# The output layer of an encoder block as seven half-size products, with sums of its weights made in DRAM

## The chip, the cores and the metric

The kernel runs on one core of a Trainium2 chip. The metric is the device time of one execution in microseconds (us). Three runs of the kernel before took 958.44 to 965.11 us, median 962.56 us. The engines are named as in the profile: PE (TensorE) multiplies matrices into PSUM, DVE (VectorE) and ACT (ScalarE) work element by element, POOL (GpSimd) does small things and issues some DMAs, SP (SyncE) issues most DMAs.

## The reference

One layer of an encoder: a token mixer, then a SwiGLU feed-forward layer, each between norms, with a residual sum. The change concerns the feed-forward layer, above all its last product:

```python
def swiglu(h, w_gate, w_up, w_down):
    return (jax.nn.silu(h @ w_gate) * (h @ w_up)) @ w_down
...
    h = rmsnorm(x, pre_ffn_gain[l])
    f = swiglu(h, w_gate[l], w_up[l], w_down[l])
    x = x + rmsnorm(f, post_ffn_gain[l])
```

Everything is float32. `h` is 1024 x 1024 (rows x features), `w_gate` and `w_up` 1024 x 2816, `w_down` 2816 x 1024.

## The kernel before

All matrices are split into a high and a low part (`split`, line 105: a cast on ACT, line 107, and a subtraction on DVE, line 110). `mm3` (line 133) multiplies in three matmuls: high x high (L135), high x low (L137), low x high (L139).

**Hidden layer (about 345 to 715 us).** There are 22 iterations `n`, alternately a block of `w_gate` (n even) and of `w_up` (n odd), for the 11 pairs of 128-wide chunks `p_` and `p_ + 11` of the 2816 features. Each iteration is already computed as seven products of half size over sums of its operands. `begin(n)` makes products 1 and 2, `rest(n)` the products 5, 6, 3, 7 and 4; each has 12 matmuls, an iteration 84. Sums of products are accumulated in one PSUM bank, and ACT copies intermediate values out (`copied`, L971) before the next product is added on top. DVE adds two of them (`plus`, L988). For even n the four results (1,1), (1,2), (2,2), (2,1) are gates (L980, L981). For odd n they are multiplied with the gates (L984), giving the activations, and POOL's DMA queue writes them ("spills") to `act_d` in DRAM (L985), 256 KB each. All these values live in `pt` tiles, 12 buffers.

The weights of iteration n come in two tiles `raw` of 512 KB (`wload`, L779 and L780 on SP's queue; three buffers). A tile is loaded when its buffer is free, which is when DVE has split or added its old contents, so DVE's order decides when a load starts. `unit1` splits the first tile (ACT's cast of `wh`), `unit2` and `unit3` form sums (L929, L733), `unit4` splits a quarter (`sh<-raw`). ACT runs its instructions in order: a cast that waits for a load holds up the copies behind it.

**Output layer (about 715 to 951 us).** For each half `dh` of the 1024 output columns, 8 PSUM banks hold the 8 row tiles `t`. For each of the 22 chunks, `operands` loads the chunk of `w_down` (`dr`, 256 KB, L1079) and of `act_d` (`ar`, 512 KB, L1081) and splits both; 8 x 3 matmuls follow. The last four chunks are taken row tile by row tile, so that a tile ends every 12 matmuls and `first_half` or `second_half` (norm, gain, residual, output DMA; L1105 to L1113) runs beside the next one. 22 x 8 x 2 x 3 = 1056 matmuls.

The code is written in program order; a scheduler orders the instructions on each engine's queue, and within a queue they run in that order.

## Time and profile before

| what | value |
|---|---|
| median of three runs | 962.56 us (958.44 to 965.11) |
| profiled execution, its own time | 964.13 us |
| span of the profiled execution | 962.3 us |
| PE busy | 945.6 us, 98% of the span |
| DVE, ACT, POOL busy | 559.6, 396.5, 87.8 us |
| DMA | 117.04 MB, mean 122 GB/s |

The profile is of one execution. Busy time is the time in which an engine had an instruction running; matmuls overlap, so 98% of busy PE means that it was never left waiting, not that it ran at its peak. A row of the timeline gives the start in us, the duration in us, the engine, the line, the operation, output<-inputs with shapes, and in square brackets the idle time just before it and what ended that.

### The profile page before, as it was taken

What the parts mean: (1) busy time and instruction counts of PE and PEld (TensorE: products, weight loads), DVE (VectorE), ACT (ScalarE), POOL (GpSimd) and SP (SyncE); (2) the same over time, 40 slices, a digit from 0 to 9 for tenths busy, and PEclk for the clock granted to TensorE, in tenths of its full rate; (3) what the DMA queues carried; (4) which work ended last, traced back from release to release, by engine and by line L of the source; (5) the groups of instructions that cost most, each with busy time, mean ns of one, the idle gap of its engine ahead of it and who ended that gap; (6) DMA issues with size and microseconds to landing.
All of it is one profiled execution on the core that took longest, in us unless ns stands there. A gap on an engine that the chain in (4) does not pass through costs nothing.

```text
span 962.3 us, 11186 instructions
## 1 busy us (share of the span) xinstructions
PE 945.6 (98%) x4240; PEld 780.7 (81%) x4240; DVE 559.6 (58%) x824; ACT 396.5 (41%) x677; POOL 87.8 (9%) x115
## 2 busy tenths in 40 slices
PE   9999999989998999999999999999999999999996
PEld 7888888878886888888888888888888888888885
DVE  4367694636588867666567656656556333533306
ACT  6433523527776534333333433333345223633201
POOL 0020113202132000000000000000000000000001
PEclk9999999989999999999999999999999999999999
DMA  8522031514246133223122221231069634254107
GB/s 331 205 67 66 6 110 45 197 66 131 88 143 223 73 121 112 75 69 129 55 77 92 95 77 66 88 110 55 33 236 328 255 132 160 79 187 165 56 1 262
DMA packets 37733, 117.04 MB, mean 122 GB/s; under 512 B 4752, under 2 KB 5424, under 8 KB 37680
## 3 DMA queue, kind: packets, MB, share of 16 engines
q1 hardware_dynamic: 31248, 95.32, 29.1%
q0 software_dynamic: 6288, 20.99, 5.6%
q8 instruction: 33, 0.54, 0.2%
q14 instruction: 20, 0.16, 0.0%
q10 hardware_dynamic: 144, 0.02, 0.0%
HBM read 94.80 MB, written 21.51 MB: 121 GB/s over the span
## 4 chain that ended last, share of the span: by engine, by line
PE 89%; DVE 4%; DMA 2%; POOL 1%; ACT 1%; issue 1%; DVEq 0%; POOLq 0%; ACTq 0%
PE ps L139 28%; PE ps L135 28%; PE ps L137 28%; PE ps L249 5%; DVE wl L110 1%; DMA t<-rg_d 1%; POOL lrs L158 1%; PE ps L189 1%; PE ps L740 1%; DMA raw<-in_x 0%; DMA raw<-in_tables 0%; DMA rg_d<-t 0%; DVE L L110 0%; ACT y L447 0%; POOL mst L851 0%
## 5 line engine op out<-in xcount | busy, mean ns | idle before, releaser
L137 PE MATMUL ps<-hl_t,sh 128*128 128x512 f32 x352 | 137.1, 389 | 0.0
L137 PE MATMUL ps<-dl,ah 128*128 128x512 f32 x352 | 137.1, 389 | 0.0
L139 PE MATMUL ps<-dh,al 128*128 128x512 f32 x352 | 137.1, 389 | 0.0
L135 PE MATMUL ps<-hh_t,sh 128*128 128x512 f32 x352 | 137.1, 389 | 0.0
L135 PE MATMUL ps<-dh,ah 128*128 128x512 f32 x352 | 137.1, 389 | 0.0
L110 DVE TENSOR_TENSOR al<-ar,ah 128x1024 fp32r<-128x1024 f32 x44 | 53.8, 1224 | 103.2 <-ACT ah L107 103.0
L110 DVE TENSOR_TENSOR t<-t,sh 128x1024 fp32r<-128x1024 f32 x42 | 51.5, 1225 | 92.5 <-ACT sh L107 92.5
L139 PE MATMUL ps<-hh_t,t 128*128 128x512 f32 x252 | 98.1, 389 | 0.0
L107 ACT CAST ah<-ar 128x1024 fp32r<-128x1024 f32 x44 | 46.0, 1051 | 111.1 <-PE ps L137 101.1
L107 ACT CAST sh<-t 128x1024 fp32r<-128x1024 f32 x42 | 44.2, 1052 | 90.0 <-PE ps L137 51.5
L988 DVE TENSOR_TENSOR pt<-ps,pt 128x512 f32<-128x512 f32 x88 | 60.4, 687 | 33.2 <-PE ps L139 32.6
L137 PEld LDWEIGHTS ps<-hl_t,sh 128*128 128x128 f32 x352 | 66.1, 188 | 13.8
L135 PEld LDWEIGHTS ps<-dh,ah 128*128 128x128 f32 x352 | 66.1, 188 | 13.8
L139 PEld LDWEIGHTS ps<-dh,al 128*128 128x128 f32 x352 | 66.1, 188 | 13.8
L135 PEld LDWEIGHTS ps<-hh_t,sh 128*128 128x128 f32 x352 | 66.1, 188 | 13.6
L137 PEld LDWEIGHTS ps<-dl,ah 128*128 128x128 f32 x352 | 66.1, 188 | 13.5
L107 ACT CAST wh<-raw 128x1024 fp32r<-128x1024 f32 x40 | 41.9, 1051 | 82.5 <-PE ps L137 21.3
L971 ACT COPY pt<-ps 128x512 f32<-128x512 f32 x88 | 51.2, 582 | 58.8 <-PE ps L139 58.8
L135 PE MATMUL ps<-hh_b,wh 128*128 128x512 f32 x176 | 69.6, 395 | 1.8 <-ACT wh L107 1.5
L139 PE MATMUL ps<-hh_b,wl 128*128 128x512 f32 x176 | 68.8, 393 | 1.0 <-DVE wl L110 1.0
L137 PE MATMUL ps<-hl_b,wh 128*128 128x512 f32 x176 | 69.3, 394 | 0.0
L135 PE MATMUL ps<-xh,wh 128*128 128x512 f32 x160 | 64.1, 401 | 0.0
(248 smaller groups left out, 1771.6 us busy)
## 6 DMA issues: line engine op xcount, KB each, us to landing
ar<-act_d SPq DMA_DIRECT2D x44, 512.0 KB, 3.7
raw<-in_w_gate SPq DMA_DIRECT2D x24, 512.0 KB, 4.0
raw<-in_w_up SPq DMA_DIRECT2D x24, 512.0 KB, 3.2
act_d<-pt POOLq DMA_DIRECT2D x44, 256.0 KB, 2.3
dr<-in_w_down SPq DMA_DIRECT2D x44, 256.0 KB, 3.7
raw<-in_w_feat SPq DMA_DIRECT2D x10, 512.0 KB, 3.7
t<-in_x SPq DMA_DIRECT2D x8, 512.0 KB, 8.6
raw<-in_w_out SPq DMA_DIRECT2D x8, 512.0 KB, 3.8
```

Of the source, the lines that this page charges most:

```text
L107: nc.scalar.copy(h, src)
L110: nc.vector.tensor_tensor(l, src, f(h), op=ALU.subtract)
L135: nc.tensor.matmul(ps, ah, bh, start=first, stop=False, skip_group_check=resumed)
L137: nc.tensor.matmul(ps, ah, bl, start=False, stop=False, skip_group_check=resumed)
L139: nc.tensor.matmul(ps, al, bh, start=False, stop=last, skip_group_check=resumed)
L158: nc.gpsimd.tensor_tensor(dst, t, mhalf[:, 0:1].broadcast_to([P, w]), op=ALU.pow)
L189: nc.tensor.matmul(warm, ones[:, 0:P], ones, start=True, stop=True)
L249: nc.tensor.matmul(uvps[t], (lk if p_ == 2 else hk)[:, ts_], (wl if p_ == 1 else wh)[:, c], start=k == 0 and p_ == 0, stop=k == NK - 1 and ...
L740: nc.tensor.transpose(tps[k // 4][:, (k % 4) * P : (k % 4 + 1) * P], hv[:, k, :], ident)
L971: copies.append(nc.scalar.copy(v, ps).ins)
L988: nc.vector.tensor_tensor(v, ps, v, op=ALU.add)
```

## The change

The output layer is computed like the hidden layer: seven products of half size instead of eight. With the activations and `w_down` cut into quarters, the left operands are `a11`, `a12`, `a22` and the sums `s3 = a11 - a21`, `s1 = a21 - a22`, `s2 = s1 - a11`, `s4 = s2 + a12`; the right operands are the quarters B11, B21, B22 and the sums `u1`, `u2`, `u3`, `u4`. Four things change:

1. In `done`, odd iterations form the four left sums on DVE (44 instructions of 128 x 512) and spill seven values per pair instead of four.
2. The right sums are made in DRAM, for six groups of two chunks (the last has one): SP copies four quarters of `w_down` into `u1`..`u4` (`copy_sums`), and POOL issues adding DMAs, two from `w_down` and two from one sum into another (`add_sums`).
3. The output layer runs seven products (`product_out`), each with 11 chunks x 4 row tiles x 3 matmuls, 924 in all. It loads 512 KB of left and 512 KB of right operand for each group of two chunks. The last two groups of a product are taken row tile by row tile.
4. The first group's operands are loaded and split during the last hidden-layer iteration (`head`). The order of two operand tiles in `hh` and `hl` is swapped, and the pools of the output layer are laid out anew.

```diff
-    act_d = drp.tile([NF, P, S], F32, name="act_d")
+    GR = [(p_, min(p_ + 2, NP)) for p_ in range(0, NP, 2)]
+    a_d = {q: grouped(q) for q in ("a11", "a12", "a22", "s1", "s2", "s3", "s4")}
+    b_d = {q: grouped(q) for q in ("u1", "u2", "u3", "u4")}
...
+    def spill(q, p_, v):
+        nc.gpsimd.dma_start(a_d[q][p_ // 2][:, (p_ % 2) * HALF : (p_ % 2 + 1) * HALF], v)
...
+        nc.vector.tensor_tensor(c, c, gates.pop((i, j)), op=ALU.mult)
+        if (i, j) == (1, 1):
+            acts["a11", p_] = c
+            spill("a11", p_, c)
+        elif (i, j) == (1, 2):
+            acts["a21"] = c
+            s3 = pt()
+            sub(s3, acts["a11", p_], c)
+            spill("s3", p_, s3)
+        elif (i, j) == (2, 2):
+            spill("a22", p_, c)
+            s1 = acts.pop("a21")
+            sub(s1, s1, c)
+            spill("s1", p_, s1)
+            s2 = acts["s2"] = pt()
+            sub(s2, s1, acts.pop(("a11", p_)))
+            spill("s2", p_, s2)
         else:
-            nc.vector.tensor_tensor(c, c, gates.pop((i, j)), op=ALU.mult)
-            nc.gpsimd.dma_start(act_d[p_ + (i - 1) * NP, :, (j - 1) * HALF : j * HALF], c)
+            spill("a12", p_, c)
+            s4 = pt()
+            nc.vector.tensor_tensor(s4, acts.pop("s2"), c, op=ALU.add)
+            spill("s4", p_, s4)
...
+    def copy_sums(g):
+        for q, w in (("u1", B11), ("u3", B12), ("u2", B22), ("u4", B21)):
+            nc.sync.dma_start(chunks(b_d[q][g]), halves_of(w, g))
+
+    def add_sums(g, q):
+        if q in ("u1", "u3"):
+            v = halves_of(B12 if q == "u1" else B22, g)
+            nc.gpsimd.dma_start(chunks(b_d[q][g]), v, accum_op=ALU.add)
+        else:
+            nc.gpsimd.dma_start(b_d[q][g], b_d["u1" if q == "u2" else "u2"][g], accum_op=ALU.add, max_dma_last_dim=1024)
...
+        if n == len(kinds) - 1:
+            head("a11", B11)
         rest(n)
+        g, j = divmod(n - 4, 3)
+        if 0 <= g < len(GR):
+            if j == 0:
+                with tc.issue_after(loads[n + 2]):
+                    copy_sums(g)
+            for q in (("u1",), ("u3", "u2"), ("u4",))[j]:
+                add_sums(g, q)
...
+        product_out("a11", B11, Xb, True, keep("v1", Xb))
+        product_out("a12", B21, Yb, True, c11)
+        product_out("s2", "u2", Xb, False, keep("u2", Xb))
+        product_out("s1", "u1", Zb, True, keep("v5", Zb))
+        product_out("s3", "u3", Xb, False, c22)
+        product_out("s4", B22, Zb, False, c12)
+        product_out("a22", "u4", Xb, False, c21)
```

How the instructions move is shown at three places. The first is DVE's queue at the end of an odd iteration, before. L988 adds products, L984 multiplies with a gate, L110 with `sh` and `raw` is the split of `unit4` that frees a `raw` buffer:

```order
L929 TENSOR_TENSOR t_696_4584<-raw_4516 128x512
L984 TENSOR_TENSOR pt_4434<-pt_4434,pt_4298 128x512
L988 TENSOR_TENSOR pt_4486<-ps_4496,pt_4486 128x512
L110 TENSOR_TENSOR sh_4512<-raw_4383,sh_4512 128x512
L984 TENSOR_TENSOR pt_4486<-pt_4486,pt_4351 128x512
L733 TENSOR_TENSOR t_696_4584<-t_696_4584,raw_4515 128x512
```

The same place now (the lines have moved: L936 was L929, L1002 was L984, L1071 was L988, L740 is a subtraction, here of `s1` and `s2`, L1022 is `s4`):

```order
L936 TENSOR_TENSOR t_717_4748<-raw_4675 128x512
L1002 TENSOR_TENSOR pt_4583<-pt_4583,pt_4446 128x512
L1071 TENSOR_TENSOR pt_4637<-ps_4652,pt_4637 128x512
L740 TENSOR_TENSOR pt_4597<-pt_4597,pt_4583 128x512
L1002 TENSOR_TENSOR pt_4637<-pt_4637,pt_4499 128x512
L740 TENSOR_TENSOR pt_4644<-pt_4597,pt_4548 128x512
L110 TENSOR_TENSOR sh_4671<-raw_4531,sh_4671 128x512
L1022 TENSOR_TENSOR pt_4668<-pt_4644,pt_4637 128x512
L740 TENSOR_TENSOR t_717_4748<-t_717_4748,raw_4674 128x512
```

Between the last sum of products and the split of `raw` stand three instructions where none stood.

The second place is POOL's queue in the iteration n = 7 and the one after it (odd, the first chunk pair of whose group is 2; in `a112_d` the tensor is `a11`, the group starts at chunk 2). L992 is a spill, L1066 an add from `w_down`, L1068 an add from one sum to another:

```order
L992 DMA a112_d_109<-pt_552_3692 128x512
L1066 DMA u12_d_151<-in_w_down 256x1x512
L1066 DMA u32_d_163<-in_w_down 256x1x512
L1068 DMA u22_d_157<-u12_d_151 512x256
L992 DMA s32_d_139<-pt_563_3766 128x512
L1068 DMA u42_d_169<-u22_d_157 512x256
L992 DMA a222_d_121<-pt_557_3727 128x512
L992 DMA s12_d_127<-pt_558_3741 128x512
L992 DMA a122_d_115<-pt_564_3781 128x512
L992 DMA s22_d_133<-pt_565_3788 128x512
L992 DMA s42_d_145<-pt_569_3812 128x512
```

Where four spills followed each other, spills now stand behind adds, and each of the last two adds reads what the add before it wrote. Groups 1, 3 and 5 are placed like this, in odd iterations; groups 0, 2 and 4 have their four adds in a row in an even iteration.

The third place is SP's queue at the copies of that group, behind the weight loads of iteration 9:

```order
L786 DMA raw_571_3818<-in_w_up 128x1024
L787 DMA raw_572_3819<-in_w_up 128x1024
L1061 DMA u12_d_151<-in_w_down 256x1x512
L1061 DMA u32_d_163<-in_w_down 256x1x512
L1061 DMA u22_d_157<-in_w_down 256x1x512
L1061 DMA u42_d_169<-in_w_down 256x1x512
L786 DMA raw_594_3960<-in_w_gate 128x1024
```

Four copies of 512 KB now stand between two weight loads, once in three iterations.

## Rows read from the trace of the kernel before

**Rows 1.** Page, parts 1 and 2: busy us, and the granted clock by slice.

```profile
PE 945.6 (98%) x4240; PEld 780.7 (81%) x4240; DVE 559.6 (58%) x824; ACT 396.5 (41%) x677; POOL 87.8 (9%) x115
...
PEclk9999999989999999999999999999999999999999
```

**Rows 2.** Page, part 4: the chain that ended last, shares by engine, by line.

```profile
PE 89%; DVE 4%; DMA 2%; POOL 1%; ACT 1%; issue 1%; DVEq 0%; POOLq 0%; ACTq 0%
PE ps L139 28%; PE ps L135 28%; PE ps L137 28%; PE ps L249 5%; DVE wl L110 1%; DMA t<-rg_d 1%; POOL lrs L158 1%; PE ps L189 1%; PE ps L740 1%; DMA raw<-in_x 0%; DMA raw<-in_tables 0%; DMA rg_d<-t 0%; DVE L L110 0%; ACT y L447 0%; POOL mst L851 0%
```

**Rows 3.** Windows: the hidden layer, the output layer, the tail, three stretches inside.

```profile
core 0: us, PE busy (x) PEld busy (x) DVE busy (x) ACT busy (x) POOL busy (x), PEclk, DMA share, GB/s
345.00:715.10 370.10, 370.10 (x1635) 306.65 (x1634) 231.27 (x314) 139.83 (x199) 21.60 (x40) 1.00 0.26 89
715.10:951.50 236.40, 236.40 (x1045) 195.87 (x1044) 96.74 (x127) 77.75 (x118) 4.35 (x8) 1.00 0.47 164
951.50:962.30 10.80, 2.61 (x12) 1.83 (x10) 4.73 (x9) 1.36 (x4) 1.08 (x2) 0.85 0.52 196
...
720.00:730.00 10.00, 10.00 (x45) 8.27 (x44) 6.17 (x8) 4.85 (x7) 0.00 (x0) 1.00 1.00 353
...
740.00:750.00 10.00, 10.00 (x46) 8.29 (x45) 4.41 (x5) 3.14 (x4) 0.00 (x0) 1.00 0.92 335
...
770.00:790.00 20.00, 20.00 (x90) 16.58 (x89) 7.30 (x8) 5.23 (x8) 0.00 (x0) 1.00 0.40 139
```

**Rows 4.** Page, part 5: the output layer's matmuls (count, busy us, mean ns).

```profile
L137 PE MATMUL ps<-dl,ah 128*128 128x512 f32 x352 | 137.1, 389 | 0.0
L139 PE MATMUL ps<-dh,al 128*128 128x512 f32 x352 | 137.1, 389 | 0.0
...
L135 PE MATMUL ps<-dh,ah 128*128 128x512 f32 x352 | 137.1, 389 | 0.0
```

**Rows 5.** Timeline, PE: product 3 of an even iteration; first and last output-layer matmul.

```profile
535.07 0.39 PE L135 MATMUL ps<-hh_b,sh 128*128 128x512 f32 x1
...
714.59 0.39 PE L135 MATMUL ps<-dh,ah 128*128 128x512 f32 x1
...
953.72 0.39 PE L139 MATMUL ps<-dh,al 128*128 128x512 f32 x1
```

**Rows 6.** Timeline, DVE: first and last of four instructions for one row tile's end.

```profile
949.49 0.22 DVE L1106 TENSOR_SCALAR fst<-fst 128x1 f32<-128x1 f32 x1 [0.44 <-ACT junk L1105]
...
951.03 0.75 DVE L1110 SCALAR_TENSOR_TENSOR fy<-fy,fst,xr 128x512 f32<-128x512 f32 x1
```

**Rows 7.** Timeline, DVE, SP and ACT: from an odd hidden-layer iteration to an even one.

```profile
525.51 0.68 DVE L988 TENSOR_TENSOR pt<-ps,pt 128x512 f32<-128x512 f32 x1
526.11 0.68 DVE L110 TENSOR_TENSOR sh<-raw,sh 128x512 fp32r<-128x512 f32 x1
...
526.82 0.33 SPq L779 DMA_DIRECT2D raw<-in_w_gate  x1
529.23 0.33 SPq L780 DMA_DIRECT2D raw<-in_w_gate  x1
546.02 0.33 SPq L779 DMA_DIRECT2D raw<-in_w_up  x1
...
530.37 1.05 ACT L107 CAST wh<-raw 128x1024 fp32r<-128x1024 f32 x1 [2.68 <-DMA raw<-in_w_gate]
...
532.55 0.59 ACT L971 COPY pt<-ps 128x512 f32<-128x512 f32 x1 [0.59 <-PE ps L139]
```

**Rows 8.** Page, part 3: SP's queue and POOL's queue (packets, MB, share of 16 engines' span).

```profile
q1 hardware_dynamic: 31248, 95.32, 29.1%
q0 software_dynamic: 6288, 20.99, 5.6%
```

**Rows 9.** Page, part 6: fastest and slowest 512 KB loads (count, size, us to landing).

```profile
raw<-in_w_up SPq DMA_DIRECT2D x24, 512.0 KB, 3.2
...
t<-in_x SPq DMA_DIRECT2D x8, 512.0 KB, 8.6
```

More of the change, by code (lines that the diff above doesn't have):

```diff
@@ new lines, in tile_encoder_layer, with head @@
+    heads = {}
+    def head(a, b):
+        rb, ra = raw(), raw()
+        get(a, b, 0, ra, rb)
+        o = []
+        for r in (rb, ra):
+            h, l = t4r(), t4r()
+            split(h, l, r)
+            o += [h, l]
+        heads[a, 0] = o
+    def copy_sums(g):
[5 more added lines that the diff above has]
+            nc.gpsimd.dma_start(chunks(b_d[q][g]), v, accum_op=ALU.add)
+        else:
+            nc.gpsimd.dma_start(b_d[q][g], b_d["u1" if q == "u2" else "u2"][g], accum_op=ALU.add, max_dma_last_dim=1024)
@@ new lines, in mm, with product_out @@
+        def mm(ps, t, o, j, first, last, resumed):
+            bh_, bl_, ah_, al_ = o
+            ts_ = slice(j * HALF + t * P, j * HALF + (t + 1) * P)
+            js = slice(j * HALF, (j + 1) * HALF)
+            mm3(ps, ah_[:, ts_], al_[:, ts_], bh_[:, js], bl_[:, js], first, last, resumed=resumed)
+        def product_out(a, b, banks, fresh, then):
+            n = len(GR)
+            for g in range(n - 2):
+                o = operands(a, b, g)
+                for j in range(2):
+                    for t in TT:
+                        mm(banks[t], t, o, j, fresh and g == 0 and j == 0, False, not fresh)
+            os = [operands(a, b, g) for g in (n - 2, n - 1)]
+            for t in TT:
+                for o, w in zip(os, (2, 1)):
+                    for j in range(w):
+                        mm(banks[t], t, o, j, False, w == 1, not fresh)
+                then(t)
```

140 lines of the change are left out of this document (83 added, 57 removed).

## The prediction

> **What bounds the kernel now.** I read the page's busy times, then the chain that ended last, then the windows, then single rows of the timeline. TensorE is busy 98% of the span at a granted clock of 9 tenths or more in every slice [rows 1]. The chain is TensorE for 89%; the three lines of `mm3` alone hold 84% [rows 2]. The windows divide this: from 345 us to 715.1 us (hidden layer) and from 715.1 us to 951.5 us (output layer) TensorE never idles, at clock 1.00; only the tail, 951.5 to 962.3 us, is something else [rows 3]. VectorE is busy 63% of the hidden layer and 41% of the output layer, ScalarE 38% and 33%, the DMA engines 26% and 47%. So a matmul taken out saves its full pitch, unless what is added makes TensorE wait where it now never does. The second question decides this case, since all the added work lies in windows where something must stay hidden.
>
> **What is removed.** The output layer has 1056 matmuls (8 row tiles, 2 halves, 22 chunks, 3 terms), three groups of 352 [rows 4]. The busy time of one, 389 ns, is no price, for they overlap. The first starts at 714.59, the last, the 1056th, at 953.72 [rows 5]: 239.13 us over 1055 steps, a pitch of 226.7 ns. Afterwards there are 7 products x 11 chunks x 4 row tiles x 3 terms = 924; the instruction lists agree, 4163 rows against 4031 on TensorE. 132 x 0.2267 = **29.9 us saved**.
>
> **What the output layer needs instead.** Each pair of chunks brings two 512 KB loads for 24 matmuls, 1.05 MB in 5.44 us, 193 GB/s. At its busiest the stage moved 353 GB/s, and later, in steady state, 139 GB/s at a DMA share of 0.40 [rows 3], so I expect a share near 0.55. Three weight and four activation buffers run ahead, and the split operands of four groups. At each product's end the lists put the splits of the next two groups (10.9 us of matmuls) ahead of the evictions, and a bank group is written again only after a whole other product (29.9 us). The first group is loaded into old weight buffers during the last hidden-layer iteration. I cost all this at nothing; the cover is the two groups.
>
> **The tail.** The last row tile's own chain is unchanged. But row tiles now end every 9 matmuls (2.04 us) instead of 12 (2.72 us), while VectorE's four instructions for one take 2.29 us from 949.49 to the end of the last, 951.03 + 0.75 [rows 6]. It falls 0.25 us behind three times: **+0.8 us**.
>
> **The hidden layer: the added VectorE work.** Four sums per pair of iterations, 44 in all. They start 0.60 us apart like their neighbours [rows 7], 26 us on an engine that idles 139 us there. What matters is what stands behind them. At the end of an odd iteration, one sum, one product and another sum now stand ahead of the split of `raw` (the order rows show it), three starts of 0.60 us, 1.8 us. That split frees the buffer into which SyncE loads the next gate weight. Before: split at 526.11, load at 526.82, ScalarE's cast of it at 530.37 after a wait, then the eviction at 532.55, which the matmul at 535.07 needs [rows 5, 7]. Cast (1.05 us) and eviction (0.59 us) must be over by 535.07, so the cast may start at 533.4 at the latest: 3.1 us of slack. The 1.8 us eat most of it; 1.3 us are left for a slower load. At the end of even iterations nothing is put ahead of the split, so up-weight loads keep their slack (taken as the same 3.1 us).
>
> **The hidden layer: the added transfers.** Per group of two chunks (57.1 us, three iterations of 84 matmuls; 5.5 groups) there are 4 DRAM copies of 256 packets, 4 adds (twice 256, twice 512 packets) and 4.5 more spills of 128. No row shows a copy inside DRAM or an add. Nearest are the queue totals [rows 8]: SyncE's queue took 29.1% of 16 engines for 31248 packets, 4480 us / 31248 = 143 ns for 3.05 KB; GpSimd's 137 ns for 3.3 KB. By bytes, 2 KB would be 94 ns and 1 KB 47 ns. Per group the copies are then 64 packets an engine, 6.0 us by bytes, 9.2 us by packets; the adds 96 packets an engine, 6.0 us by bytes, 13.7 us by packets, 27.5 us if each costs double, as it reads its destination too; the spills 36 packets, 4.9 us. With the 26% that is there (14.8 us) the share of DMA time comes to 0.56 at the low end and 0.99 at the high end; I take the packet price of the rows, undoubled, 42.6 of 57.1 us, 0.75.
>
> The Trainium skill ("Collectives: The Full Stack", "The bandwidth ceiling: the fold count and why AG ≠ RS ≠ AR") says that a DMA add costs twice a copy, because it sends two reads per chunk through the ring, and not because of the adding. No row here can show it. By it the sum would be the doubled one, 0.99.
>
> What does this cost TensorE? A gate load is 128 packets, 8 an engine. If each waits for one foreign packet it lands 8 x 0.143 = 1.1 us later (2.3 us if doubled). It overlaps two spills today; four afterwards. 1.1 us fits into the 1.3 us that are left, though barely. In three of the eleven pairs the last add of a group and the spills queued behind it on GpSimd meet a gate load; I charge half a microsecond for each: **+1.5 us**; bounds 0 and, at the doubled price in all eleven pairs, 11 x (1.8 + 2.3 + 0.5 - 3.1) = 16.5 us (0.5 us for the two extra spills).
>
> GpSimd waits for each add to land before the next one that reads it, and spills wait behind. It idled before; what counts are the `pt` buffers that the spills free. The iteration of [rows 7] began 48 matmuls before 535.07, at 524.2; copies follow the second weight load, 5 us in, and land some 3.5 us later (as the load did, 526.82 to 530.37), so the adds start about 8.5 us into an odd iteration. The last one of a group is issued two landings later, then five spills go. The buffer of the first is wanted again by the next pair (two iterations, 38.1 us, and 14 us into its second), 52 us in. So an add may take (52 - 8.5 - 3) / 2 = 20 us, with 3 us for the spill itself; landings of 512 KB seen here are 3.2 to 8.6 us [rows 9]. I cost this at nothing.
>
> **Sum.** 964.13 us (the profiled execution: span 962.3 and 1.8 around it) - 29.9 + 0.8 + 1.5 = 936.5 us. The runs shown have a median 1.6 us lower; I say **936 us**.
>
> **Rivals.**
> 1. *DMA contention eats half.* For it: 0.75 to 0.99 of the engines' time, and 1.3 us of slack. Against: early in the output layer the share was 1.00 and 0.92 and TensorE did not stop [rows 3]. Price: the upper bound, 936.5 - 1.5 + 16.5 = 951.5 us; the typical case lies at 942 to 951.
> 2. *Slower: the copies hold up SyncE's queue.* They stand on that queue right behind a weight load; the next weight load follows 16.8 us later (529.23 to 546.02, [rows 7]) with 3.1 us of slack, and finds 64 packets an engine ahead of it. Free up to 20 / 64 = 0.31 us a packet. The gain is gone when each of 5.5 groups loses 5.3 us, at 0.40 us a packet. At 0.60 us it is 5.5 x 18.4 = 101 us lost, about 1035 us. Against: 0.143 us in the nearest row. For: no row has both ends in DRAM, in 2 KB pieces.
> 3. *No change: adds land slowly.* At 25 us a landing, the spills behind the last add go (8.5 + 50 + 3) - 52 = 9.5 us too late in each of the three odd groups, 28.5 us: 964 us. It decides from 20 us upwards. Against: the 8.6 us.
> 4. *The output layer waits for its loads.* At under 169 GB/s (1.05 MB in the 6.2 us that would undo the saving) nothing is gained: 964 us. Against: 353 GB/s.
>
> The Trainium skill ("DMA: Bandwidth & Descriptors", "Issuing engines are not separate DMA queues") says that DMAs of all issuers run on the same 16 engines and interleave, so moving the adds to GpSimd's queue shelters nothing. That is rival 1's mechanism; the trace has one DMA share for all queues and can't show it apart.
>
> **Chances.** Forecast (931 to 941 us) 0.70; rival 1 0.14; rival 2 0.08; rival 3 0.05; rival 4 0.03. About 1% (9.6 us) is what a measurement of this kernel tells from no change. Faster by over 1%: forecast and nearly all of rival 1, 0.83; within 1%: rivals 3 and 4 with an edge of rival 1, 0.08; slower: rival 2 and a worse rival 3, 0.09. The range goes from 930 us (no stall at all; the runs before reach 4 us below their median) to 950 us, which takes in rival 1 nearly to its bound: 0.82. All cases but 0.17 have one sign, so no second range is given.
>
> **What would show it.** Windows: hidden layer still 370 us with TensorE busy throughout; output layer 924 matmuls in about 209 us at a DMA share near 0.55; tail 11 to 12 us. In the waits: ScalarE waiting for `raw` of w_gate, longer by 1 to 2 us than the 2.7 us of today, without idle TensorE behind it. Wrong if TensorE shows idle time after a ScalarE copy in the hidden layer (rival 1 or 2: by whether w_gate loads alone or both kinds land late), if copies land later than 15 us (2), if an add lands later than 20 us (3), or if the output layer idles for a load (4).

## The result, and the profile after

The changed kernel took 936.26 us (median; the kernel before beside it 961.2 us), a ratio of 0.9727 (95% interval 0.9675 to 0.9779). In a second set on another chip it took 937.27 against 961.71 us: 0.9748 (0.9721 to 0.9775). It is faster by 2.5 to 2.7%; 936 us was forecast. Left out as slow executions are 1866.52 us of the changed kernel, in whose trace the matmuls of both layers come 0.44 to 0.56 us apart at a granted clock of 1.00, and 1939.87 and 1046.62 us of the kernel before, which have no trace. The profile shown is that of the second set (`after_again`), whose own time is 936.75 us.

The page of the profiled execution, parts 1 and 4: busy us of each engine, then the chain that ended last, by engine and by line.

```profile
PE 914.3 (98%) x4108; PEld 751.7 (80%) x4108; DVE 603.9 (65%) x876; ACT 406.5 (43%) x677; POOL 131.6 (14%) x172
...
PE 48%; issue 3%; DMA 3%; DVE 2%; ACT 1%; POOL 0%; DVEq 0%; POOLq 0%; ACTq 0%
PE ps L135 16%; PE ps L139 16%; PE ps L137 16%; DMA raw<-in_w_gate 2%; ACT sh L107 1%; DVE t L110 1%; DVE pt L1071 1%; DVE pt L1002 0%; ACT pt L978 0%; DVE pt L740 0%; ACT wh L107 0%; DVE sh L110 0%; DMA out<-fy 0%; DVE fy L1228 0%; POOL fs
```

Before, the chain was TensorE for 89% and no load of `w_gate` stood among its lines [rows 2]. Now loads of `w_gate` are in it, and the VectorE and ScalarE lines of the hidden layer around them. (The two shares of TensorE do not compare: the chain is followed back to the start of the span before, and now only to 399.85 us, so its shares add up to some 57%.) The windows (columns as in [rows 3]) say where that is: hidden layer, output layer, tail.

```profile
345.00:718.60 373.60, 368.17 (x1616) 302.46 (x1615) 255.41 (x352) 139.60 (x199) 62.16 (x93) 1.00 0.63 175
718.60:927.90 209.30, 209.30 (x926) 173.27 (x924) 115.88 (x140) 87.34 (x120) 7.29 (x12) 1.00 0.63 212
927.90:934.90 7.00, 0.37 (x2) 0.00 (x0) 3.82 (x7) 0.69 (x2) 0.83 (x2) 0.89 0.57 211
```

In the hidden layer TensorE is now idle for 5.4 us (373.60 against 368.17), which it never was [rows 3], and the DMA share has gone from 0.26 to 0.63. In the output layer it still never idles. The time by stages, from the starts of single matmuls in the timeline (hidden layer: from its first matmul with `hh_t,sh` to the first of the output layer; tail: from the last matmul's start to the end of the span):

| stage | before | after | difference |
|---|---|---|---|
| up to the hidden layer | 325.63 | 322.13 | -3.50 |
| hidden layer | 388.96 | 396.54 | **+7.58** |
| output layer | 239.13 | 209.21 | **-29.92** |
| tail | 8.58 | 7.02 | **-1.56** |
| span | 962.3 | 934.9 | -27.4 |

The span is read to 0.1 us, so a tail is good to 0.05 us. The change adds no work to the first stage. Its end moves from profile to profile: 324.7 to 327.3 us in the three that have the old output layer, 319.8 to 325.2 us in the ten that have the new one. The granted clock there goes with it for the most part (200 to 220 us: 0.84 to 0.90 in the three, 0.90 to 1.00 in the ten). Whether the order of instructions has a part in this was not tried. Kernels are compared below by the three other stages and by medians over runs: the three stages give -23.9 us, the medians -24.4 and -24.9 us, so the first stage is worth at most 1 us in the median.

Most of the idle time lies in five gaps. (A gap is the time from one matmul's start to the next one's where that is longer than the 0.227 us of the pitch; the five are 1.84, 1.58, 1.46, 1.75 and 0.65 us.) The timeline of PE has the matmul behind each, with the idle time and what ended it in brackets:

```profile
399.90 0.50 PE L135 MATMUL ps<-hh_b,sh 128*128 128x512 f32 x1 [1.45 <-ACT pt L978]
420.44 0.50 PE L135 MATMUL ps<-hh_b,sh 128*128 128x512 f32 x1 [1.19 <-ACT pt L978]
459.88 0.50 PE L135 MATMUL ps<-hh_b,sh 128*128 128x512 f32 x1 [1.07 <-ACT pt L978]
576.43 0.50 PE L135 MATMUL ps<-hh_b,sh 128*128 128x512 f32 x1 [1.36 <-ACT pt L978]
615.11 0.50 PE L135 MATMUL ps<-hh_b,sh 128*128 128x512 f32 x1 [0.26 <-ACT pt L978]
```

Each is the first matmul of its iteration's product 3, as that of 535.07 in [rows 5], and each waited for ScalarE's eviction. The first gap stands in an odd iteration (up weights), the others in even ones. The chain of waits around the second one shows why:

```profile
411.33 0.69 DVE pt L740
412.02 0.62 DVE sh L110
412.64 0.02 issue
412.65 6.13 DMA raw<-in_w_gate
...
418.86 0.22 ACT wh L107
419.08 0.74 issue
419.81 0.59 ACT pt L978
420.40 0.04 issue
420.44 0.50 PE ps L135
```

It is read from the end: the matmul of 420.44 waits for the eviction (`pt`), the eviction stands behind ScalarE's cast of `wh`, the cast waited for the gate load, the load took 6.13 us (before: 526.82 to 530.37, 3.55 us, [rows 7]) and started late, because VectorE's split (`sh`, L110) of the buffer stood behind `s2` (L740).

What was in flight meanwhile stands in the timelines of SP, ACT and POOL. Ahead of the third stall (gate load, cast, then POOL's DMA issues):

```profile
452.22 0.33 SPq L786 DMA_DIRECT2D raw<-in_w_gate  x1
...
458.30 1.05 ACT L107 CAST wh<-raw 128x1024 fp32r<-128x1024 f32 x1 [3.04 <-DMA raw<-in_w_gate]
...
449.56 1.02 POOL L1068 DMA_DIRECT2D u_d<-u_d  x1 [5.76 <-DMA u_d<-in_w_down]
450.20 0.98 POOL L992 DMA_DIRECT2D s_d<-pt  x1
456.64 1.05 POOL L1068 DMA_DIRECT2D u_d<-u_d  x1 [5.46 <-DMA u_d<-u_d]
457.28 0.99 POOL L992 DMA_DIRECT2D a_d<-pt  x1
457.85 0.98 POOL L992 DMA_DIRECT2D s_d<-pt  x1
```

The load was issued with a whole add in flight (issued 449.56; the next one, which waits for it to land, 456.64) and its cast started 6.08 us later. The fourth stall is the same: add issued 566.18 and landed 572.90, gate load issued 568.48, cast 574.85. Ahead of the first stall it was the up-weight load, issued at 390.21, behind two adds issued at 388.48 and 389.62: its cast started at 398.32, 8.1 us later, where up-weight loads took 3.2 to 3.4 us before. The second and the fifth are of another kind: ahead of the second the last add had landed at 411.42, 1.2 us before the gate load was issued, and both loads met spills alone.

### The profile page after: what moved, and what is told of

Its sections match the earlier page's. It is cut to its first block, busy times and chain, and to the rows that moved or that the text cites. A ratio compares the mean times of both kernels' runs of the same rounds, so it can differ in the third digit from the quotient of the medians.

```text
span 1864.7 us, 11122 instructions
## 1 busy us (share of the span) xinstructions
PE 1857.7 (100%) x4108; PEld 1205.5 (65%) x4108; DVE 609.5 (33%) x876; ACT 408.8 (22%) x677; POOL 134.2 (7%) x172
## 3 DMA queue, kind: packets, MB, share of 16 engines
q0 software_dynamic: 17760, 41.18, 8.1%
## 4 chain that ended last, share of the span: by engine, by line
PE 99%; issue 0%; DVE 0%; ACT 0%; DVEq 0%; POOLq 0%; POOL 0%; ACTq 0%
PE ps L135 31%; PE ps L139 31%; PE ps L137 31%; PE ps L256 5%; PE ps L747 1%; PE ps L196 0%; PE ps L460 0%; PE ps L432 0%; PE ps L697 0%; PE ps L324 0%; PE ps L143 0%; PE ps L144 0%; PE ps L147 0%; PE ps L411 0%; DVE fy L1228 0%
## 5 line engine op out<-in xcount | busy, mean ns | idle before, releaser
L135 PE MATMUL ps<-hh_t,sh 128*128 128x512 f32 x352 | 237.4, 674 | 0.0
L137 PE MATMUL ps<-hl_t,sh 128*128 128x512 f32 x352 | 237.3, 674 | 0.0
L137 PE MATMUL ps<-ol,oh 128*128 128x512 f32 x300 | 202.4, 675 | 0.0
L135 PE MATMUL ps<-oh,oh 128*128 128x512 f32 x300 | 202.3, 674 | 0.0
L139 PE MATMUL ps<-oh,ol 128*128 128x512 f32 x300 | 202.3, 674 | 0.0
L1071 DVE TENSOR_TENSOR pt<-ps,pt 128x512 f32<-128x512 f32 x88 | 60.7, 689 | 269.1 <-PE ps L139 216.0
L110 DVE TENSOR_TENSOR t<-t,sh 128x1024 fp32r<-128x1024 f32 x42 | 51.5, 1225 | 254.2 <-ACT sh L107 254.2
L110 DVE TENSOR_TENSOR ol<-ar,oh 128x1024 fp32r<-128x1024 f32 (+1 forms) x41 | 46.4, 1132 | 242.5 <-ACT oh L107 242.5
L137 PEld LDWEIGHTS ps<-ol,oh 128*128 128x128 f32 x300 | 89.5, 298 | 50.9 <-issue 47.4
L135 PEld LDWEIGHTS ps<-oh,oh 128*128 128x128 f32 x300 | 89.3, 298 | 50.8 <-issue 46.5
L139 PEld LDWEIGHTS ps<-oh,ol 128*128 128x128 f32 x300 | 89.3, 298 | 50.6 <-issue 47.2
L137 PE MATMUL ps<-xl,wh 128*128 128x512 f32 x160 | 110.0, 688 | 0.0
L139 PE MATMUL ps<-xh,wl 128*128 128x512 f32 x160 | 109.4, 683 | 0.0
```

Source lines behind the costliest of these rows:

```text
L110: nc.vector.tensor_tensor(l, src, f(h), op=ALU.subtract)
L135: nc.tensor.matmul(ps, ah, bh, start=first, stop=False, skip_group_check=resumed)
L137: nc.tensor.matmul(ps, ah, bl, start=False, stop=False, skip_group_check=resumed)
L139: nc.tensor.matmul(ps, al, bh, start=False, stop=last, skip_group_check=resumed)
L1071: nc.vector.tensor_tensor(v, ps, v, op=ALU.add)
```

## The experiments

Times are medians; ratios are against the kernel before on the same chip, with 95% intervals; stages are read from one profile of each kernel, as in the table above. How far such a reading can be trusted shows in `tail_15`: its hidden layer has the changed kernel's instructions in the same order on every engine, and it took 2.2 us less.

| kernel | us | ratio | hidden layer | tail |
|---|---|---|---|---|
| before | 960.3 to 963.2 | 1 | 388.96 | 8.58 |
| changed (`after_again`) | 937.27 | 0.9748 (0.9721, 0.9775) | 396.54 | 7.02 |
| `no_sums` | 932.21 | 0.9697 (0.9673, 0.9721) | 390.21 | 7.09 |
| `no_sums_split` | 930.50 | 0.9681 (0.9662, 0.9699) | 389.31 | 7.00 |
| `copies_only` | 935.22 | 0.9707 (0.9680, 0.9733) | 391.06 | 7.03 |
| `plain` | 935.33 | 0.9735 (0.9714, 0.9757) | 394.62 | 7.78 |
| `split_first` | 934.16 | 0.9736 (0.9708, 0.9764) | 393.31 | 7.06 |
| `spread` | 936.94 | 0.9749 (0.9725, 0.9773) | 395.10 | 7.00 |
| `tail_15` | 933.51 | 0.9709 (0.9684, 0.9734) | 394.34 | 6.61 |
| `best` | 929.70 | 0.9686 (0.9660, 0.9713) | 390.17 | 6.54 |
| `best2` | 931.06 | **0.9664** (0.9643, 0.9685) | 389.32 | 6.60 |
| `before_xr` | 962.18 | 0.9989 (0.9970, 1.0008) | 388.96 | 8.53 |
| `before_spills` | 961.60 | 0.9988 (0.9970, 1.0005) | 388.96 | 6.84 |

The output layer took 209.21 or 209.22 us in every kernel that has the seven products.

**The changed kernel again** (no edit).

> The changed kernel itself, for a profile at the usual pace (the one profiled before ran at double the matmul pitch throughout) and more timings. Theory of the prediction: about 936 us; hidden layer 370 us with TensorE busy throughout, output layer 924 matmuls in about 209 us at a DMA share near 0.55, tail 11 to 12 us, TensorE at a pitch of 226.7 ns. Rival 1 (contention on the DMA engines): the same time, but by accident: idle TensorE in the hidden layer after a ScalarE copy, made up for somewhere else, say by a faster front part or a shorter tail. In the rows: a copy inside DRAM lands in under 15 us, an add in under 20 us (in the run at double pitch 7.3 us and 5.8 to 8.2 us by the median), at the usual pace somewhat more.

Measured: 937.27 us, rival 1's picture: the time as forecast, but with the stalls shown above, made up for by a shorter tail and a shorter first stage. Output layer 209.21 us, as forecast, at a DMA share of 0.63. Copies land in 7.4 us, adds in 8.9 us (out of `w_down`) and 6.9 us (sum to sum), by the page's part 6.

**Without copies and adds.**

```diff
-                    copy_sums(g)
+                    pass
...
-                add_sums(g, q)
+                pass
...
-        product_out("s2", "u2", Xb, False, keep("u2", Xb))
+        product_out("s2", B22, Xb, False, keep("u2", Xb))
```

(and so for `u1`, `u3` and `u4`).

> The changed kernel without its 24 copies inside DRAM and 24 adding DMAs; the four products that read the sums read quarters of w_down in their place (so the right sums are left out of what is computed). Everything on TensorE, VectorE and ScalarE stands in the same order. Theory of the prediction: the copies and adds cost TensorE at most the 1.5 us that I charged: 0 to 1.5 us faster than the changed kernel, ScalarE's wait for w_gate loads 0 to 1 us shorter. Rival 1: 6 to 15 us faster, with TensorE's idle time in the hidden layer gone.

Measured: the hidden layer 390.21 us, so copies and adds cost 6.33 us there, four times what I charged. By the ratios it is 0.51% or 4.9 us: over the theory's 1.5 us, and short of rival 1's 6 to 15. Two gaps are left, both ahead of the same matmul:

```profile
420.79 0.50 PE L135 MATMUL ps<-hh_b,sh 128*128 128x512 f32 x1 [0.24 <-ACT pt L978]
...
497.32 0.50 PE L135 MATMUL ps<-hh_b,sh 128*128 128x512 f32 x1
```

The first comes 0.63 us after the matmul ahead of it, the second 0.42 us, instead of 0.227. Gate loads take 4.5 to 5.3 us here from issue to cast, 3.6 to 3.8 us in the kernel before (once 4.4), up-weight loads 3.2 to 3.4 us in both. So the five spills that now stand within 3 us of a gate load's issue cost it some 1.1 us, and a load of 5.0 us or more, issued 1.8 us late, is what it takes to stop TensorE.

**Without copies and adds, sums behind the split.** The edit to `done` and `rest` of this kernel and of the next one:

```diff
         elif (i, j) == (2, 2):
             spill("a22", p_, c)
-            s1 = acts.pop("a21")
-            sub(s1, s1, c)
...
+            acts["a22"] = c
         else:
-            spill("a12", p_, c)
...
+            acts["a12"] = c
+
+    def left_sums(n):
...
         unit4(n + 1)
         wload(n + 2)
+        left_sums(n)
```

> The kernel without copies and adds (four products read quarters of w_down where the sums stood), and with s1, s2 and s4 formed behind the split that frees the weight buffer. Theory: without copies and adds, what is left of the loss in the hidden layer is 1.2 us, and it comes from the 1.8 us by which three VectorE sums delay the split; so here the hidden layer takes 389.0 us as in the kernel before, no gap in TensorE's matmuls, and the time is 0.5 to 1.5 us below that without sums alone. Rival: the 1.2 us come from the extra spills that share the DMA engines with the gate load: no difference to the kernel without sums.

Measured: the hidden layer 389.31 us, 0.35 us over the kernel before, no gap over 0.34 us. By the ratios 0.16% or 1.5 us less than without sums alone, the intervals overlapping. The rival falls as it was put: the same number of spills is there. But they moved with the sums: of the five, four were issued ahead of the gate load in `no_sums` and one here (at the load of 486.34 us), and gate loads now take 3.6 to 4.2 us. So this run takes away the delay and part of what the load meets. More spills without the delay leave no stall either (`before_spills`, below); the delay without the added spills was not run. The 1.25 us came from the two together, as far as this shows.

**Sums behind the split, with copies and adds.**

> The changed kernel with the sums s1, s2 and s4 formed at the end of an odd iteration, behind the split that frees the weight buffer, so that the gate load starts as early as it did in the kernel before. Theory of the prediction: the 1.8 us by which the sums delay the load lie within ScalarE's slack of 3.1 us, so the time is the same within 1.5 us, and only ScalarE's wait for w_gate loads is 1.5 to 2 us shorter each. Rival 1: the delay costs TensorE; 5 to 16 us faster (11 pairs by 0.5 to 1.5 us).

Measured: hidden layer 393.31 us, 3.2 us less than in the changed kernel; by the ratios 0.12%, which is not told from nothing. So the time came out as the theory said (within 1.5 us), and the profile's 3.2 us is little above the 2.2 us by which two profiles of the same instructions differ. What the profile does show is that three gaps of 1.0 to 2.1 us remain where an add was in flight, though the gate load was issued 1.8 us earlier: taking away the delay is not enough.

**Copies without adds.**

```diff
-                add_sums(g, q)
+                pass
```

> The changed kernel with its 24 copies inside DRAM but without the 24 adding DMAs (so the right sums are not formed). It divides the 6.3 us that copies and adds cost together in the hidden layer (7.6 us lost in the changed kernel's profile, 1.2 us without both). Theory: it is the adds, and the spills that they hold back on GpSimd's queue until the next weight load is in flight, that make the loads late, since copies are issued right behind a load and have landed 11 us before the next: loss in the hidden layer 1.2 to 2 us, time near that without sums (932 us). Rival 2 in its weak form: the copies themselves hold up the next loads; loss 4 us or more, time 935 us or more, and up-weight loads that take longer than 3.4 us.

Measured: 935.22 us, not near 932 as expected, but on a chip on which the kernel before took 963.18 us; by the ratios 0.10% over `no_sums` and 0.41% or 4.0 us under the changed kernel. Hidden layer 391.06 us, so the copies cost 0.85 us beside `no_sums` and the adds 5.5 us. The only gap over 0.34 us:

```profile
418.93 0.50 PE L135 MATMUL ps<-hh_b,sh 128*128 128x512 f32 x1 [1.19 <-ACT pt L978]
```

The gate load ahead of it was issued at 411.15, took 6.2 us, and only spills stood beside it; the copies had been issued 30 us earlier. So what the copies cost is not told from what spills do alone. This is the load ahead of the changed kernel's second gap, and it takes 6.2 us there too: that gap is not the adds' doing. It is the slowest gate load beside spills in every kernel that has the delay (5.3 us in `no_sums`, 7.1 in `plain`, 7.2 in `spread`), and 4.4 us in the kernel before; why stays open. Up-weight loads take 3.1 to 3.5 us, 3.2 us also for the one issued at 390.46 with a copy in flight until 391.71. Rival 2 falls in its weak form too.

**Adds turned into plain copies.**

```diff
-            nc.gpsimd.dma_start(chunks(b_d[q][g]), v, accum_op=ALU.add)
+            nc.gpsimd.dma_start(chunks(b_d[q][g]), v)
```

(and so for sum to sum).

> The changed kernel with the 24 adding DMAs turned into plain copies of the same shape on the same queue (so the right sums are not formed). If an add costs the DMA engines twice a copy, as the doubled price of the prediction had it: the landings of these 24 fall from 8.9 us (out of w_down) and 6.9 us (sum to sum) by a third or more, GpSimd's queue takes clearly less of the engines' time than the 16.9% of the changed kernel (8.2% of it are there without the adds), and the loss in the hidden layer falls from 7.6 us to 4 to 6 us. If an add costs what a copy costs: landings, share and loss are the same within a tenth, and the time is 936 to 938 us.

Measured: part 3 of the page, GpSimd's queue (packets, MB, share of 16 engines' span), in the changed kernel, as plain copies, and without either:

```profile
q0 software_dynamic: 17760, 41.18, 16.9%
```

```profile
q0 software_dynamic: 12128, 41.18, 12.1%
```

```profile
q0 software_dynamic: 8928, 29.65, 8.2%
```

(Packets count the 4-byte ones that tell of a landing.) Share x span x 16 engines: 2528, 1811 and 1222 us. The 24 DMAs take 1306 us as adds and 589 us as copies of the same bytes, 2.2 times as much. They also land sooner:

```profile
u_d<-in_w_down POOLq DMA_DIRECT2D x10, 512.0 KB, 8.9
u_d<-u_d POOLq DMA_DIRECT2D x10, 512.0 KB, 6.9
```

```profile
u_d<-in_w_down POOLq DMA_DIRECT2D x10, 512.0 KB, 6.1
u_d<-u_d POOLq DMA_DIRECT2D x10, 512.0 KB, 4.7
```

Yet the hidden layer loses 5.66 us instead of 7.58, and the time by the ratios falls by 0.13%, within the intervals. The add costs the DMA engines twice the copy, and that is not the main thing here: a load that meets plain copies of 512 KB on GpSimd's queue is late too. The up-weight load of 392.16 met two and took 7.4 us (gap 1.12 us), the gate load of 569.06 met one and took 6.4 us (gap 1.77 us). The worst gap, 2.48 us, is not of this kind: its gate load (413.87, 7.1 us) met spills alone, the last copy having landed at 406.34. The adds come in 8832 packets and the copies in 3200, so the mean packet of an add is not dearer (148 against 184 ns), but it is smaller. The packet records tell the sizes apart: the adds out of `w_down` came in 2 KB packets of 204 ns in the mean, the adds of sum to sum in 1 KB packets of 127 ns, and SyncE's copies out of `w_down` into the same tensors in 2 KB packets of 90 to 92 ns (`copies_only`, 381 to 393 and 436 to 449 us). At equal size and between the same ends, an add's packet took 2.2 times a copy's.

**Copies and adds given out over 17 iterations.**

```diff
-        g, j = divmod(n - 4, 3)
-        if 0 <= g < len(GR):
-            if j == 0:
-                with tc.issue_after(loads[n + 2]):
-                    copy_sums(g)
...
+        if 3 <= n <= 19:
+            some = [SUMS.pop(0) for _ in range(min(len(SUMS), 1 if n % 2 else 2))]
+            with tc.issue_after(loads[n + 2]):
+                for s in some:
+                    copy_sum(*s)
+            for g, q, w in some:
+                add_sums(g, q)
```

> The changed kernel with the same 24 copies and 24 adds given out over 17 hidden-layer iterations, one of each in an odd one and two in an even one, each copy behind that iteration's weight loads, where the changed kernel issues four copies at once in every third iteration. New theory, from the trace of the changed kernel (five gaps of 0.65 to 1.84 us between matmuls in the hidden layer, each behind a ScalarE cast that waited for a weight load that took 5.3 to 8.1 us from issue to cast instead of 3.2 to 3.8 us): it is not the amount of transfers but that loads meet copies and adds in flight that costs 5 us. Then no copy or add is in flight when a load is issued 19 us later, the gaps are those of the kernel without sums (1.2 us in all, where the changed kernel loses 7.6 us), and the time is 4 to 6 us below the changed kernel, near 932 us. Rival: the amount counts, and what is taken from one load is given to another: 936 to 938 us, with the loss spread over more iterations.

Measured: 936.94 us, nothing gained; the hidden layer still loses 6.1 us. But nearly all of it (5.7 us) is lost in the first two iterations with copies and adds, at 401.53 and 423.10 us, and not a gap over 0.34 us stands behind 427 us, in the other fifteen:

```profile
401.53 0.50 PE L135 MATMUL ps<-hh_b,sh 128*128 128x512 f32 x1 [1.32 <-ACT pt L978]
...
423.10 0.79 PE L135 MATMUL ps<-hh_b,sh 128*128 128x512 f32 x1 [2.23 <-ACT pt L978]
423.69 0.63 PE L137 MATMUL ps<-hl_b,sh 128*128 128x512 f32 x1
```

At the first, two adds issued at 390.89 and 392.06 met the up-weight load of 392.77, which took 7.2 us: that load follows the one before it by 12.8 us, where 17 us and more lie between them later. So there was not the room that the theory counted on. Nor is its wording right, that no add is in flight when a load is issued: the up-weight load of 512.13 was issued 1.1 us after an add, took 5.8 us and left no gap. The second gap's gate load (414.27) took 7.2 us beside spills alone, as in `copies_only` and `plain`.

**The last product's last three groups by row tile.**

```diff
-            os = [operands(a, b, g) for g in (n - 2, n - 1)]
+            os = [operands(a, b, g) for g in range(n - last, n)]
...
-        product_out("a22", "u4", Xb, False, c21)
+        product_out("a22", "u4", Xb, False, c21, 3)
```

> The changed kernel with the last three groups, not two, of the last product taken row tile by row tile: row tiles end 15 matmuls (3.40 us) apart where they end 9 matmuls (2.04 us) apart in the changed kernel. Theory of the prediction: VectorE's 2.29 us for one row tile's end fit again, so 0.8 us faster (0 to 1), since it is no longer behind at the last one. Rival: the tail is set by the last row tile's own chain and VectorE is not behind there: no difference; or the splits of three groups must all stand ready earlier, and TensorE waits: 1 to 3 us slower.

Measured: the tail 6.61 us, 0.41 us shorter. VectorE's instructions for a row tile now start 3.40 us apart and wait for ScalarE, where in the changed kernel they follow on one another. The first instruction of each row tile's end in the changed kernel, VectorE's timeline:

```profile
922.97 0.22 DVE L1221 TENSOR_SCALAR fst<-fst 128x1 f32<-128x1 f32 x1 [9.02 <-ACT junk L1220]
...
925.17 0.21 DVE L1221 TENSOR_SCALAR fst<-fst 128x1 f32<-128x1 f32 x1
...
927.36 0.21 DVE L1221 TENSOR_SCALAR fst<-fst 128x1 f32<-128x1 f32 x1
...
929.55 0.21 DVE L1221 TENSOR_SCALAR fst<-fst 128x1 f32<-128x1 f32 x1
```

Starts 2.19 to 2.20 us apart with no wait, against 2.04 us of matmuls: 0.15 us behind with each of three, 0.46 us in all. The median is 3.8 us lower, more than the tail explains; the rest lies in the hidden layer (394.34 us, two stalls fewer, with the same instructions there), which the edit does not touch, and in the spread of the runs.

**Residual rows loaded earlier in the kernel before.**

```diff
             nc.scalar.copy(m0[:, t, :], ps)
+            XR[t] = finp.tile([P, D], F32, tag="xr", name=nm("xr"), bufs=8)
+            nc.sync.dma_start(XR[t], x1_d[t * P : (t + 1) * P, :])
...
-            xr = finp.tile([P, D], F32, tag="xr", name=nm("xr"), bufs=4)
-            nc.sync.dma_start(xr, x1_d[t * P : (t + 1) * P, :])
+            xr = XR[t]
```

> The kernel before, with the eight 512 KB loads of residual rows (xr) issued during the output layer's first half, into eight buffers, where four of them were issued among the output writes of the last 25 us. It tests what shortened the tail in the changed kernel (8.6 us from the last matmul's start to the end of the span before, 7.0 us after), which the prediction had longer by 0.8 us. Theory: the last output write landed late because loads and writes together kept the DMA engines at a share of 0.86 to 0.99 until the end; then this kernel's tail is 1.5 to 2.5 us shorter, 6.1 to 7.1 us, its last writes land in 2.0 to 2.5 us, and the time is 1.5 to 2.5 us below the kernel before. Rival: the tail is set by the rate of the writes alone (one row tile in 2.72 us); tail unchanged within 0.5 us.

Measured: the writes land in 2.0 us by the median (3.0 us before, though the last two took 2.0 us there already), and the tail is still 8.53 us. My theory of the shorter tail fell. What ended the span shows when the instructions named DRAIN at the program's end are listed (count, shortest, median and longest ns, first and last start). Before, then with earlier rows, then the changed kernel, then the changed kernel without sums:

```profile
L1238 POOLq DRAIN  x3: 40/93/6309, 955.2 to 962.0; - x3
```

```profile
L1240 POOLq DRAIN  x3: 40/102/6311, 954.2 to 961.1; - x3
```

```profile
L1376 POOLq DRAIN  x3: 46/93/3734, 929.8 to 934.7; - x3
```

```profile
L1376 POOLq DRAIN  x3: 40/93/1409, 926.5 to 931.4; - x3
```

Before, GpSimd's drain began at 955.2 and ended 6.31 us later, at 961.5, some 2 us after the last write had landed; the rest of the program's end follows it. In the changed kernel the drain is over at 929.8 + 3.73 = 933.5, ahead of the last landing. In `plain`, whose drain took 5.09 us, the tail is 0.8 us longer again.

**More spills in the kernel before.**

```diff
             nc.gpsimd.dma_start(act_d[p_ + (i - 1) * NP, :, (j - 1) * HALF : j * HALF], c)
+            if (i, j) != (2, 1):
+                nc.gpsimd.dma_start(more_d[p_ + (i - 1) * NP, :, (j - 1) * HALF : j * HALF], c)
```

> The kernel before with 33 more spills on GpSimd's queue in the hidden layer (three of four values of a pair are also written to a second DRAM tensor that nothing reads), so that GpSimd issues as many DMAs in all, 102, as the changed kernel without copies and adds. It tests what shortened the tail: GpSimd's last drain took 6.31 us in the kernel before and ended its span, 1.41 us in the changed kernel without copies and adds, 3.73 us in the changed kernel, while earlier residual loads left it at 6.31 us and the tail at 8.5 us. Theory: the drain's length goes with what GpSimd has issued on its DMA queue before, not with the output layer; here it is shorter than 6.31 us (near 1.41 us if only the number counts), the tail falls from 8.6 to about 7.2 us, and the hidden layer loses 0 to 1 us to the spills. Rival: the drain belongs to the old output layer (its 16 output writes in a row): 6.3 us again, tail 8.5 to 8.6 us.

Measured: the drain takes 1409 ns, the tail 6.84 us, with the old output layer unchanged:

```profile
L1241 POOLq DRAIN  x3: 40/102/1409, 956.8 to 961.9; - x3
```

So the old tail was 1.7 us longer than it had to be, for a reason that lies in what GpSimd had issued some 240 us and more earlier. The time changes by 0.12% (interval -0.05% to 0.30%), as 1.7 us would and as nothing would. The hidden layer, 388.96 us, shows no stall with the spills alone; gate loads take 4.2 to 4.7 us.

**Placement, split and tail together.** The edits of `spread`, `split_first` and `tail_15` in one kernel.

> The whole computation, with three changes to the changed kernel together: copies and adds given out over the iterations, the sums s1, s2 and s4 behind the split, and the last product's last three groups taken row tile by row tile. Theory: the hidden layer loses nothing against the kernel before (389 us from its first to the output layer's first matmul, where the changed kernel takes 396.5), the tail is 0.4 us shorter than in the changed kernel: 7.5 to 8 us below the changed kernel's profile at an equal front part, some 929 to 931 us. Rival: the transfers left in the way of the loads still cost; 933 to 936 us.

Measured: 929.70 us, as expected; hidden layer 390.17 us, 1.2 us over the kernel before where nothing was expected; tail 6.54 us. One gap is left, at 399.10 us, ahead of which two adds were issued at 388.94 and 390.12 beside the up-weight load of 390.53 (7.0 us).

**The same, beginning two iterations later.**

```diff
-        if 3 <= n <= 19:
-            some = [SUMS.pop(0) for _ in range(min(len(SUMS), 1 if n % 2 else 2))]
+        if 5 <= n <= 19:
+            some = [SUMS.pop(0) for _ in range(min(len(SUMS), (2 if n == 19 else 1) if n % 2 else (4 if n == 18 else 2)))]
```

> As the kernel with the three changes together (copies and adds given out, s1, s2 and s4 behind the split, last three groups by row tile), but the first copy and add stand two iterations later, behind the weights of iteration 7; four stand together near the end instead. In that kernel the one gap that was left (0.94 us) came at the second of the early iterations, where the DMA engines were at a share of 0.92 to 1.05 for 12 us even ahead of the load. Theory: with the start moved, the up-weight load of that iteration takes 3.2 us as in the kernel without sums, no gap, hidden layer 389.0 to 389.5 us; 928 to 929.5 us. Rival: the four at the end give the gap back there; 929.5 to 931 us.

Measured: no gap over 0.34 us; hidden layer 389.32 us, 0.36 us over the kernel before, with all copies and adds in it. Windows of hidden layer, output layer and tail:

```profile
345.00:709.40 364.40, 364.40 (x1608) 301.25 (x1607) 252.47 (x350) 139.54 (x198) 63.25 (x93) 1.00 0.64 179
709.40:918.60 209.20, 209.20 (x924) 173.28 (x923) 117.56 (x142) 87.28 (x119) 7.61 (x12) 1.00 0.64 214
918.60:925.20 6.60, 0.39 (x2) 0.00 (x0) 2.31 (x5) 0.69 (x2) 0.54 (x1) 0.68 0.42 159
```

TensorE never idles at a DMA share of 0.64, which is the changed kernel's 0.63: the amount of transfers was not the trouble, where they stood was. They still meet loads. One up-weight load was issued 1.2 us after an add and took 6.4 us, and no gap followed:

```profile
539.56 1.02 POOL L1077 DMA_DIRECT2D u_d<-u_d  x1 [4.95 <-DMA u_d<-u_d]
...
540.78 0.33 SPq L786 DMA_DIRECT2D raw<-in_w_up  x1
...
547.19 1.05 ACT L107 CAST wh<-raw 128x1024 fp32r<-128x1024 f32 x1 [5.69 <-DMA raw<-in_w_up]
```

The up-weight loads that were followed by a gap had met two adds (7.0 to 8.1 us in `best`, `spread`, `split_first` and the changed kernel). The ratio is 0.9664 (0.9643 to 0.9685) against 0.9748 (0.9721 to 0.9775) for the changed kernel, 0.84% or 8 us better, and the intervals do not touch. The median of 931.06 us lies above the 928 to 929.5 us expected and above that of `best`, on a chip on which the kernel before took 963.18 and not 960.34 us; against `best` the ratio is 0.22% lower, within the intervals.

## Why the prediction was right, and where it was wrong

The time came out as forecast, 936 us, and the mechanism of the large term was right. Two other terms were wrong, with opposite signs, so that the time met the forecast to within 1.3 us is luck. The prediction's own sign of being wrong appeared: TensorE idle after a ScalarE copy in the hidden layer, with loads of both kinds late. Rival 1 held there, at 6 us and not at 15.

- **The matmuls taken out.** 132 at the old pitch, 29.9 us; measured 239.13 - 209.21 = 29.92 us.
- **The output layer's loads.** Hidden, as costed, at 0.63 of DMA time and 212 GB/s, where I had expected 0.55 and 193. Rival 4 fell.
- **VectorE's sums ahead of the split.** I had 1.8 us of delay, 1.1 us for a load beside four spills, and 3.1 us of slack. Measured in `no_sums`: the split starts 2.41 us after the last sum of products instead of 0.60 (as at 409.53 and 411.94 in the changed kernel), 1.81 us; gate loads 1.1 us longer; gaps once a load reaches 5.0 us, 1.3 us over its 3.7 us of before. The three numbers were right, and 1.25 us lost is what it looks like when they add up to about the slack.
- **Copies and adds in the hidden layer, the step that failed.** "In three of the eleven pairs the last add of a group and the spills queued behind it on GpSimd meet a gate load; I charge half a microsecond for each": +1.5 us. They cost 6.3 us by the profiles, of which 5.5 us are the adds', and 4.9 and 4.0 us by the ratios. I had let a load wait for one foreign packet for each of its own, 1.1 us. Beside a whole add in flight a gate load took 6.1 and 6.4 us instead of 3.7, in two of the three pairs named; behind the third no gate load is left. The spills that I had queued behind the add were not what it met: they were issued from 457.28 us on, when the load of 452.22 had all but landed. And I had given the up-weight loads no loss. Their 3.1 us of slack was about right (6.4 us left no gap in `best2`), but the one that met two adds took 8.1 us and cost 1.6 us by itself. The second gap, 1.4 us, stands beside spills alone and is not explained. The bound of rival 1 (16.5 us) was not passed, and its reach of 942 us was missed only because of the next two points.
- **The tail, also wrong.** +0.8 us was forecast, -1.56 us measured. VectorE does fall behind, by 0.46 us (the last of the four instructions starts 0.08 us ahead of the end of the one before it, and row tiles start 2.19 us apart and not 2.29). But the old tail was ended by GpSimd's drain, which I had not looked at; it was no part of the row tile's chain, which I called unchanged.
- **What made up the sum.** Forecast for the three stages -27.6 us, measured -23.9 us. The profiled execution came to 936.75 us because its first 322 us, to which the change adds no work, were 3.5 us shorter than in the profile before. I had read [rows 1] as a clock of 9 tenths or more in every slice; the ninth slice has 8, and 200 to 220 us had 0.88 before and 1.00 after. By the medians the saving was 24.4 to 24.9 us where 26.5 was forecast (962.56 to 936), and the kernel before was itself 1 us faster in these sets.
- **DMA price and share.** The share in the hidden layer is 0.63, between my 0.56 and 0.75. The adds take 1306 us / 16 / 5.5 = 14.8 us a group, where I had 13.7 by packets. The count of packets was right; the flat 143 ns came near by accident, since it lies between the 204 ns of an add's 2 KB and the 127 ns of its 1 KB. As copies the same bytes take 6.7 us, near my 6.0 by bytes, so doubling the price by bytes (12.0 us) came near as well. The Trainium skill ("Collectives: The Full Stack", "The bandwidth ceiling: the fold count and why AG ≠ RS ≠ AR") says of collectives in a ring that the step that adds sends two reads per chunk where a copy sends one, and so reaches half the bandwidth. Here, with no collective, an add took 2.2 times a copy by engine time for the same bytes, which agrees in size; no run shows the reads.
- **Rivals 2 and 3.** Copies land in 7.4 us (wrong from 15), adds in at most 8.9 us by the median (wrong from 20), and the one weight load issued while a copy was still in flight took 3.2 us without adds (`copies_only`).

## What to carry to other kernels

A transfer that nothing waits for still has a price when it is in flight at the moment at which a load with little slack is issued: ask for each added DMA what else is issued within its landing time, not what share of the engines it takes. Put such transfers right behind the tight load, a few at a time, and form nothing ahead of the instruction that frees that load's buffer. Here, with the sums behind the split, the hidden layer took 389.31 us without copies and adds, 393.31 us with the 24 copies and 24 adds in one place and 389.32 us with them in another. When a stage is shortened, look at what ends the old one: part of the tail belonged to no step of the computation.

## What the runs showed of the hardware that I had not expected

- GpSimd's drain at the end of the program took 6.31 us in the kernel before, 1.41 us with 33 more spills, 1.41 us in the changed kernel without adds, 3.73 to 3.98 us with adds and 5.09 us with plain copies in their place; the packets on its queue were 6288, 8928, 8928, 17760 and 12128. It changed with what was issued on the queue alone (`before_spills`), but it does not grow or fall with the amount; by what rule stays open.
- After the gap of 2.62 us in `spread`, with TensorE idle for 2.23 us, the next seven matmuls came 0.42 to 0.59 us apart instead of 0.227. The records have a granted clock of 0.50 there, the lower of TensorE's two levels (1.2 GHz), from 423.08 us for 3.41 us; the windows below show it as a mean of 0.69. That stall cost some 1.7 us beyond its length. After the changed kernel's gaps of up to 1.84 us the next matmul came 0.34 us later, and after the 2.48 us in `plain` (2.09 us idle) the clock stayed at 1.00.

```profile
420.00:424.00 4.00, 1.77 (x6) 1.19 (x5) 1.22 (x1) 2.48 (x4) 0.00 (x0) 0.89 0.78 296
424.00:428.00 4.00, 4.00 (x14) 3.12 (x14) 1.43 (x2) 0.48 (x1) 2.15 (x2) 0.69 0.42 44
```
